# Delta-rule layer: a half-size inverse layout, and 512-column matmuls for every block but the gates

## The chip, the cores and the metric
The kernel runs on one core of one Trainium2 chip. The metric is the device time of one execution in microseconds (us). The kernel before takes 2532.01 us (median of 3 runs, 2531.71 to 2532.07). Five engines work side by side from queues of their own: TensorE (PE in the profile, its weight loads are PEld), VectorE (DVE), ScalarE (ACT), GpSimd (POOL) and SyncE (SP), which issues the weight transfers.

## The reference
Two layers over 256 tokens of width 2048, float32: differential attention and a gated MLP with a causal convolution, then a gated delta-rule layer and a second such MLP. Only the delta-rule layer changes. Its core, cut to what matters:

```python
proj = h @ w_in                                   # q, k, v, z, and two gate columns per head
qkv = silu(causal_dwconv(qkv, conv_w))            # 4 taps
q, k = l2_norm(q), l2_norm(k)
# per head and chunk of 64 tokens:
low = strict_lower(k_beta @ k.T * decay)
u, w = solve(I + low, v_beta), solve(I + low, k_beta * exp(g))
...                                               # scan over the 4 chunks with a state
o = rms_norm(o, norm_g) * silu(z)
x = x + o @ w_out
```

There are 16 q/k heads and 32 value heads of 128 columns. The kernel solves with an explicit inverse of unit lower triangular matrices: first all diagonal blocks of 32x32 by elimination on DVE, then the off-diagonal blocks by small matmuls.

## The kernel before, in words
Every large product is done in float32 precision with two halves of each operand. A weight chunk of 128x1024 numbers lands by DMA in `raw`; ACT rounds it to `whi` (L89) and DVE subtracts to get `wlo` (L90). The activations stand as a high half and a low half side by side, 2 x 256 columns. Each of `raw`, `whi`, `wlo` has four buffers.

`dense` (L132) multiplies one weight block of 256 output rows: for each of the k tiles and each of two row tiles it runs one *step*. A step in the **wide** form is two matmuls: high weights over all 512 activation columns (L151), whose low-activation half goes to its own 256 columns of the PSUM bank, and low weights over the 256 high-activation columns (L152). A step in the **narrow** form is three matmuls of 256 columns, all into the same 256 columns of PSUM: L151, L152, and the high weights loaded again for the low activations (L154). After a wide block the two column halves of the bank must still be added: in `lin` ACT copies the small half (L580), DVE adds the main half (L581) and scales by the row norm (L205); after a narrow block DVE scales directly out of PSUM (L196). In `out`, a wide block costs two additions to `x` on DVE (`add_x`, L343), a narrow one costs one. Two PSUM tiles `ps` take turns, so a block's bank pair must be read before the block after the next begins.

`gdn` (L542) goes through four groups of four q/k heads (b = 0..3). Per group: four `k` blocks (q and k of one head, 16 k tiles each), one `v` block, two `z` blocks in the other orientation (`dense_tok`, L207), three more `v` blocks, and then the eight output blocks of the group before (`out`, L818, 8 k tiles each). The last group's output blocks follow at the end.

All other work is spread between the weight chunks by generators: after every chunk `tick` (L71) advances each live generator to its next `yield`. So a `yield` means "one weight chunk later" in program order. `keys` (L594) squares and splits q and k, sums over the head by matmul, normalises, multiplies q and k and writes the diagonal blocks, by POOL copies (L650), into `Cc`. `invert` (L654) transposes `Cc` on DVE into `X` (L659), fills `Ti` with minus `X` and ones on the diagonal (L661, L662), runs 30 elimination steps of a multiply (L667) and a subtract (L670), and transposes the result twice (`ttc` L674, `tcc` L676). `levels` (L679) builds the larger inverse with small matmuls and POOL copies, and `group` (L752) applies it and makes the operand `oc` of the output blocks. A scheduler keeps program order as priority, with the compile-time readiness of each instruction; on the chip every engine runs its own list in the fixed order that results.

In `Ti`, 128 partitions hold four quadrants of 32 rows; the 32 partitions of a quadrant are 32 matrices, of which 16 are real (8 value heads x 2 half sequences) and 16 are zero. Elimination step j works on (31-j) x j numbers per partition.

Of the kernel before, what the change touches and what calls it, by code (L numbers as in the profile page):

```python
# [16 lines left out]
P = 128  # L17
T = 256
D = 2048
KD = D // P  # L20
# [6 lines left out]
class Trunk:  # L27
# [514 lines left out]
    def gdn(self, w_gate, w_in, w_z, w_out, nb, hb, gate_ap, const_ap, conv_col, ng, done):  # L542
# [7 lines left out]
        nc, tc, mp = self.nc, self.tc, self.mp  # L550
        nq = nb * hb
# [3 lines left out]
        with tc.tile_pool(name="gd", bufs=1) as gd:  # L555
# [3 lines left out]
            ident, mask = con[:, :P], con[:, P:]  # L559
# [9 lines left out]
                nc.gpsimd.memset(Tas[i][:64], 0.0)  # L569
            quad = [slice(32 * s, 32 * s + 32) for s in range(4)]  # L570
            flat = "p i c -> p (i c)"
            gates, lows = {}, []

            def lin(w, wide):
# [19 lines left out]
            def keys(hq, c, cc, b0, res):  # L594

                sq = gd.tile([P, 2, T], F32, tag="qs", name="qs", bufs=2)
                nc.scalar.square(sq, c)
                sp = gd.tile([P, 2, 2, T], F32R, tag="qp", name="qp", bufs=1)
                lows.append(self.split(sp, sq))

                def fetch():
                    d = gd.tile([P, 2, 384], F32, tag="lt", name="lt", bufs=hb)
                    nc.sync.dma_start(d, gates["rows"][2 * hq:2 * hq + 2, :].unsqueeze(0).to_broadcast([P, 2, 384]))
                    return d

                d = fetch() if "rows" in gates else None
                yield
                yield
                while "rows" not in gates:
                    yield  # L610
                if d is None:
                    d = fetch()
                    yield
                    yield
                    yield
                gc = gates["col"]
                dv = d[:, :, :T].rearrange("p v (t c) -> p v t c", t=2)
# [12 lines left out]
                nc.vector.tensor_tensor(c, c, sq, ALU.mult)  # L630
                q, k = c[:, 0, :], c[:, 1, :]
                yield
                yield
                prods = []
                for r in (k, q):
                    p = mp()
                    nc.tensor.matmul(p[:, :P], k[:, P:], r[:, P:], start=True, stop=True)
                    nc.tensor.matmul(p[:, P:384], k[:, :P], r, start=True, stop=True)  # L638
                    prods.append(p)
                lt = d  # L640
                qkt = gd.tile([P, 2, 384], F32, tag="qkt", name="qkt", bufs=hb)
                for v in range(2):
                    nc.vector.scalar_tensor_tensor(
                        qkt[:, v], prods[1][:, :384], P ** -0.5, d[:, v], ALU.mult, ALU.mult)
                    nc.vector.tensor_tensor(lt[:, v], prods[0][:, :384], d[:, v], ALU.mult)
                for v in range(2):
                    b = b0 + v
                    lv = lt[:, v, :T].rearrange("p (t c) -> p t c", t=2)
                    for r in quad:
                        nc.gpsimd.tensor_copy(  # L650
                            cc[r, :, 2 * b:2 * b + 2].rearrange("p c t -> p t c"), lv[r, :, r])
                    res.append((lt[:, v], qkt[:, v]))

            def invert(cc, lqs, inv):  # L654

                while len(lqs) < 2 * hb:
                    yield
                x = gd.tile([P, 32, 32], F32, tag="s4", name="X", bufs=3)
                nc.vector.transpose(x.rearrange(flat), cc.rearrange(flat))  # L659
                t = gd.tile([P, 32, 32], F32, tag="s4", name="Ti", bufs=3)  # L660
                nc.vector.tensor_scalar(t, x, -1.0, None, ALU.mult)  # L661
                nc.vector.memset(t.rearrange(flat)[:, ::33], 1.0)  # L662
                for j in range(1, 31):
                    m = 31 - j
                    tmp = gd.tile([P, T], F32, tag="tmp", name="tmp", bufs=1)
                    w = tmp[:, :m * j].rearrange("p (i c) -> p i c", c=j)
                    nc.vector.tensor_tensor(  # L667
                        w, x[:, j + 1:, j:j + 1].to_broadcast([P, m, j]),
                        t[:, j:j + 1, :j].to_broadcast([P, m, j]), ALU.mult)
                    nc.vector.tensor_tensor(t[:, j + 1:, :j], t[:, j + 1:, :j], w, ALU.subtract)  # L670
                    if j % 3:
                        yield
                ttc = gd.tile([P, 32, 32], F32, tag="s4", name="ttc", bufs=3)
                nc.vector.transpose(ttc.rearrange("p m i -> p i m"), t)  # L674
                tcc = gd.tile([P, 32, 32], F32, tag="s4", name="tcc", bufs=3)
                nc.vector.transpose(tcc.rearrange("p m c -> p c m"), t.rearrange("p i c -> p c i"))  # L676
                inv += [ttc, tcc]

            def levels(lqs, inv, gs, done):  # L679
# [137 lines left out]

            def out(b, acts):  # L818
                for blk in range(KD // 2):
                    wide = b == nb - 1 or blk >= KD // 4  # L820
                    ps = self.dense(w_out[b * (KD // 2) + blk], 2 * hb, lambda k: self.await_(acts, k), wide=wide)
                    self.add_out(blk, ps, done if b == nb - 1 else None, wide)

# [2 lines left out]
            pend = None  # L826
            for b in range(nb):
                heads = range(b * hb, (b + 1) * hb)
                cc = gd.tile([P, 32, 32], F32, tag="s4", name="Cc", bufs=3)
                nc.gpsimd.memset(cc, 0.0)  # L830
                lqs, inv, solved, acts, zts = [], [], [], [], {}
                groups = [range(i, i + gh) for i in range(0, hb, gh)]
                plan = [("k", i) for i in range(hb)] + [("v", 0)] + [("z", g) for g in range(len(groups))]
                for op, i in plan + [("v", i) for i in range(1, hb)]:
                    if op == "k":
                        hq = heads[i]
                        c = convs(lin(w_in[hq * 2], False), (hq, nq + hq))
                        self.spawn(keys(hq, c, cc, 2 * i, lqs))
                        if i == hb - 1:
                            self.spawn(invert(cc, lqs, inv))  # L840
                            self.spawn(levels(lqs, inv, range(len(groups)), solved))
                    elif op == "z":
                        gr = groups[i]
                        zt = zts[i] = gd.tile([P, 2, gv, P], F32, tag="vz", name="zt", bufs=4)
                        ps = self.dense_tok(w_z[heads[gr[0]] // 2], KD, self.h_acts)
                        for t in range(2):
                            nc.scalar.activation(zt[:, t].rearrange(flat), ps[:, t, :], AF.Silu,  # L847
                                                 scale=self.rstdc[:, t:t + 1])
                    else:
                        gi = i // gh  # L850
                        gr = groups[gi]
                        if i == gr[0]:
                            vt = gd.tile([P, 2, gv, P], F32, tag="vz", name="vt", bufs=4)
                            ready = []
                            self.spawn(group(gi, gr, lqs, solved, vt, ready, zts, acts))
                        hq = heads[i]
                        c = convs(lin(w_in[hq * 2 + 1], b<nb-1),
                                  (2 * nq + 2 * hq, 2 * nq + 2 * hq + 1))
                        self.spawn(to_tokens(c, vt, 2 * (i - gr[0]), ready))
                if pend:  # L860
                    out(*pend)
                pend = (b, acts)
# [213 lines left out]
```

## Time and profile before

| | |
|---|---|
| median of 3 runs | 2532.01 us |
| profiled execution | 2531.32 us, its span 2529.5 us |
| PE, PEld busy | 2522.4 us (100%), 2330.5 us (92%) |
| DVE, ACT, POOL busy | 1913.4 us (76%), 1501.8 us (59%), 97.2 us (4%) |
| chain that ended last | PE 99%, DMA 1% |
| weights read | 482.32 MB, 192 GB/s over the span |

In the lines of groups a row reads: line, engine, operation, output<-inputs, shapes, count | busy us in all, mean ns of one | idle time of the engine before them, and who ended it. Matmuls are pipelined: a matmul's own duration in the profile is longer than the distance to the next one, so the cost of a step is read from the distance between starts in the timeline. The delta-rule layer lies between about 1050 us and 1850 us of the span.

### The profile page before, as it was taken

Reading aid. Unit: us, or ns where it says so; the run is one execution under the profiler, and the core shown is the slowest. Engines: PE = TensorE matmul, PEld = TensorE weight load, DVE = VectorE, ACT = ScalarE, POOL = GpSimd, SP = SyncE. Lnnn points to the kernel's source line nnn. Section 1 sums busy time; section 2 is a strip of 40 time slices with the busy share of each in tenths; the row PEclk is TensorE's granted clock in tenths of the full one; section 3 lists DMA queues with packets and bytes.
Section 4 is the critical chain, followed back from the end, with each engine's and each line's share of the span. In section 5 each row is a group of like instructions: output and inputs, shape, how many; then the busy total and the mean of one; then the engine's idle time right before and its main releaser. Section 6 shows DMA issues by size and latency. Waiting matters only on the chain.

```text
span 2529.5 us, 42709 instructions
## 1 busy us (share of the span) xinstructions
PE 2522.4 (100%) x16727; PEld 2330.5 (92%) x16727; DVE 1913.4 (76%) x2822; ACT 1501.8 (59%) x2082; POOL 97.2 (4%) x189
## 2 busy tenths in 40 slices
PE   9999999999999999999999999999999999999999
PEld 8998899999999999999989989999999999999998
DVE  8886677777777555689879789788787777776544
ACT  7766656666666444485674675674566666665343
POOL 0000000000000000011110021021000000000000
PEclk9999999999999999999999999999999999999999
DMA  7555566666666666666555555555466666666665
GB/s 257 175 183 175 167 204 201 201 201 201 201 201 202 201 199 201 203 189 207 163 170 197 162 183 190 163 186 174 162 201 200 202 201 201 201 202 205 210 207 157
DMA packets 138203, 487.25 MB, mean 193 GB/s; under 512 B 15473, under 2 KB 18449, under 8 KB 138001
## 3 DMA queue, kind: packets, MB, share of 16 engines
q1 hardware_dynamic: 137712, 484.17, 60.0%
q8 instruction: 131, 2.15, 0.4%
q14 instruction: 72, 0.58, 0.1%
q10 hardware_dynamic: 288, 0.35, 0.0%
HBM read 482.32 MB, written 2.15 MB: 192 GB/s over the span
## 4 chain that ended last, share of the span: by engine, by line
PE 99%; DMA 1%; DVE 0%; ACT 0%; SPq 0%; issue 0%; ACTq 0%
PE ps L151 50%; PE ps L152 27%; PE ps L154 4%; PE ps L221 3%; PE ps L220 3%; PE ps L222 3%; PE mp L765 2%; PE mp L151 1%; PE mp L329 1%; PE mp L638 1%; PE mp L152 0%; PE ps L123 0%; PE mp L730 0%; PE mp L748 0%; PE mp L810 0%; PE mp L466 0%
## 5 line engine op out<-in xcount | busy, mean ns | idle before, releaser
L90 DVE TENSOR_TENSOR wlo<-raw,whi 128x1024 fp32r<-128x1024 f32 (+2 forms) x911 | 1102.6, 1212 | 510.2 <-ACT whi L89 502.0
L89 ACT CAST whi<-raw 128x1024 fp32r<-128x1024 f32 (+2 forms) x911 | 944.1, 1038 | 849.9 <-PE ps L151 627.1
L151 PE MATMUL ps<-h,whi 128*128 128x512 f32 (+1 forms) x4208 | 1348.0, 366 | 0.0
L152 PE MATMUL ps<-h,wlo 128*128 128x256 f32 x4208 | 1151.2, 274 | 0.6 <-DVE wlo L90 0.6
L151 PEld LDWEIGHTS ps<-h,whi 128*128 128x128 f32 x4208 | 797.2, 189 | 93.6 <-ACT zt L847 0.2
L152 PEld LDWEIGHTS ps<-h,wlo 128*128 128x128 f32 x4208 | 807.7, 192 | 2.0 <-DVE wlo L90 0.9
L151 PE MATMUL ps<-ac,whi 128*128 128x512 f32 x1546 | 506.8, 382 | 0.0
L152 PE MATMUL ps<-ac,wlo 128*128 128x256 f32 x1546 | 421.2, 273 | 0.0
L151 PEld LDWEIGHTS ps<-ac,whi 128*128 128x128 f32 x1546 | 292.1, 189 | 40.6 <-PE ps L151 0.2
L152 PEld LDWEIGHTS ps<-ac,wlo 128*128 128x128 f32 x1546 | 296.8, 192 | 0.1
L154 PE MATMUL ps<-h,whi 128*128 128x256 f32 x656 | 181.8, 277 | 0.0
L151 PE MATMUL ps<-oc,whi 128*128 128x512 f32 (+1 forms) x512 | 159.7, 344 | 0.0
L220 PE MATMUL ps<-whi,h 128*128 128x512 f32 x384 | 146.4, 381 | 0.0
L221 PE MATMUL ps<-wlo,h 128*128 128x512 f32 x384 | 145.8, 380 | 0.0
L222 PE MATMUL ps<-whi,h 128*128 128x512 f32 x384 | 145.8, 380 | 0.0
L310 DVE SCALAR_TENSOR_TENSOR cv<-u,fcols,cv 128x255 f32<-128x255 f32 (+1 forms) x344 | 142.9, 477 | 0.0
L152 PE MATMUL ps<-oc,wlo 128*128 128x256 f32 x512 | 140.7, 275 | 0.0
L154 PEld LDWEIGHTS ps<-h,whi 128*128 128x128 f32 x656 | 125.8, 192 | 0.2
L151 PEld LDWEIGHTS ps<-oc,whi 128*128 128x128 f32 x512 | 97.4, 190 | 8.0
L152 PEld LDWEIGHTS ps<-oc,wlo 128*128 128x128 f32 x512 | 98.3, 192 | 0.3
L308 ACT ACTIVATE cv<-u,fcols 128x256 f32<-128x256 f32 x172 | 93.9, 593 | 0.6 <-DVE u L205 0.5
L310 DVE SCALAR_TENSOR_TENSOR cv<-u,cols,cv 128x255 f32<-128x255 f32 (+2 forms) x192 | 84.2, 478 | 0.4 <-ACT cv L306 0.3
(222 smaller groups left out, 2178.7 us busy)
## 6 DMA issues: line engine op xcount, KB each, us to landing
raw<-w_up SPq DMA_DIRECT2D x344, 512.0 KB, 4.7
raw<-w_down SPq DMA_DIRECT2D x160, 512.0 KB, 3.7
raw<-w_in SPq DMA_DIRECT2D x128, 512.0 KB, 4.6
raw<-w_z SPq DMA_DIRECT2D x64, 512.0 KB, 3.8
raw<-w_out SPq DMA_DIRECT2D x64, 512.0 KB, 4.3
raw<-w_qk SPq DMA_DIRECT2D x56, 512.0 KB, 4.6
raw<-w_v SPq DMA_DIRECT2D x32, 512.0 KB, 3.5
raw<-w_o SPq DMA_DIRECT2D x32, 512.0 KB, 4.7
```

What stands on the lines that cost most here:

```text
L89: self.cast = nc.scalar.copy(hi[:, :, s], raw[:, :, s])
L90: nc.vector.tensor_tensor(lo[:, :, s], raw[:, :, s], hi[:, :, s].bitcast(F32), ALU.subtract)
L151: nc.tensor.matmul(bank[c][:, :n], hi[:, k, s], self.turns(a[:, :n // T, :]), start=first, stop=False)
L152: nc.tensor.matmul(bank[c][:, :T], lo[:, k, s], self.turns(a[:, :1, :]), start=False, stop=last and wide)
L154: nc.tensor.matmul(bank[c][:, :T], hi[:, k, s], self.turns(a[:, 1:, :]), start=False, stop=last)
L220: nc.tensor.matmul(ps[:, c, :], ah, wh, start=first, stop=False)
L221: nc.tensor.matmul(ps[:, c, :], ah, wl, start=False, stop=False)
L222: nc.tensor.matmul(ps[:, c, :], al, wh, start=False, stop=last)
L308: nc.scalar.activation(out, u, AF.Identity, bias=bias, scale=taps[n - 1])
L310: nc.vector.scalar_tensor_tensor(out[:, j:], u[:, :T - j], taps[n - 1 - j], out[:, j:], ALU.mult, ALU.add)
L329: last = self.nc.tensor.matmul(out, self.onesr, self.pairs(p[:, j]), start=i + j == 0, stop=i + j == n)
L765: nc.tensor.matmul(p[:, v, :], l(v), r[:, v, :], start=i == 0, stop=i == len(terms) - 1)
```

## The change
Two things change in `gdn`.

First, the inverse. `Cc` holds only the 16 real matrices per quadrant (`nl = 4 * hb`). The transpose into `X` reads them twice over, so that partitions 0 to 15 of a quadrant and partitions 16 to 31 hold the same 16 matrices. `Ti` is 32x16: the first half of the partitions holds the even columns of the inverse, the second half the odd ones. Elimination step j, now for j = 0..30, works on (31-j) x (j//2+1) numbers. `Ti` starts as a unit pattern (a POOL memset of 512 columns and two POOL copies of 16 columns from a small tile `half`, which DVE makes once), so the fill by DVE goes. The final transposes are of 512 columns instead of 1024, and `ttc` is made from `tcc`. The memset of `Cc` goes. Each of these tiles gets a buffer of its own where five shared three.

Second, the widths. All `k` blocks, the last group's `v` blocks, and the first four output blocks of groups 0 to 2 go from narrow to wide. Only the gate block stays narrow. `keys` waits one more `yield` before it goes on.

```diff
@@ keys
-                yield
-                yield
+                for _ in range(3):
+                    yield
@@ invert
+                while not lqs:
+                    yield
+                if b == 0:
+                    nc.vector.tensor_reduce(half, ident.rearrange("p (q a c) -> p a q c", q=4, a=2), AX.XY, ALU.add)
+                t = gd.tile([P, 32, 16], F32, tag="Ti", name="Ti")
+                nc.gpsimd.memset(t, 0.0)
+                for a in range(2):
+                    nc.gpsimd.tensor_copy(t.rearrange(flat)[:, 16 * a::33], half[:, a:a + 1].to_broadcast([P, 16]))
                 while len(lqs) < 2 * hb:
                     yield
-                x = gd.tile([P, 32, 32], F32, tag="s4", name="X", bufs=3)
-                nc.vector.transpose(x.rearrange(flat), cc.rearrange(flat))
-                t = gd.tile([P, 32, 32], F32, tag="s4", name="Ti", bufs=3)
-                nc.vector.tensor_scalar(t, x, -1.0, None, ALU.mult)
-                nc.vector.memset(t.rearrange(flat)[:, ::33], 1.0)
-                for j in range(1, 31):
-                    m = 31 - j
+                x = gd.tile([P, 32, 32], F32, tag="X", name="X")
+                nc.vector.transpose(x, cc.unsqueeze(2).to_broadcast([P, 32, 2, nl]))
+                for j in range(31):
+                    m, n = 31 - j, j // 2 + 1
...
-                ttc = gd.tile([P, 32, 32], F32, tag="s4", name="ttc", bufs=3)
-                nc.vector.transpose(ttc.rearrange("p m i -> p i m"), t)
-                tcc = gd.tile([P, 32, 32], F32, tag="s4", name="tcc", bufs=3)
-                nc.vector.transpose(tcc.rearrange("p m c -> p c m"), t.rearrange("p i c -> p c i"))
+                tcc = gd.tile([P, nl, 32], F32, tag="tcc", name="tcc")
+                nc.vector.transpose(tcc.rearrange("p m (c a) -> p c a m", a=2), t.rearrange("p i c -> p c i"))
+                ttc = gd.tile([P, nl, 32], F32, tag="ttc", name="ttc")
+                nc.vector.transpose(ttc.rearrange(flat), tcc.rearrange(flat))
@@ out
-                    wide = b == nb - 1 or blk >= KD // 4
+                    wide = True
@@ the loop over groups
-                cc = gd.tile([P, 32, 32], F32, tag="s4", name="Cc", bufs=3)
-                nc.gpsimd.memset(cc, 0.0)
+                cc = gd.tile([P, 32, nl], F32, tag="Cc", name="Cc")
...
-                        c = convs(lin(w_in[hq * 2], False), (hq, nq + hq))
+                        c = convs(lin(w_in[hq * 2], True), (hq, nq + hq))
...
-                        c = convs(lin(w_in[hq * 2 + 1], b<nb-1),
+                        c = convs(lin(w_in[hq * 2 + 1], True),
```

More of the change, by code (lines that the diff above doesn't have):

```diff
@@ L571, in gdn @@
             flat = "p i c -> p (i c)"
+            nl = 4 * hb
+            half = gd.tile([P, 2], F32, tag="half", name="half")
             gates, lows = {}, []
@@ L652, in keys, with invert @@
                     res.append((lt[:, v], qkt[:, v]))
-            def invert(cc, lqs, inv):
+            def invert(b, cc, lqs, inv):
+                while not lqs:
[6 more added lines that the diff above has]
+                    nc.gpsimd.tensor_copy(t.rearrange(flat)[:, 16 * a::33], half[:, a:a + 1].to_broadcast([P, 16]))
@@ L665, in invert @@
+                nc.vector.transpose(x, cc.unsqueeze(2).to_broadcast([P, 32, 2, nl]))
+                for j in range(31):
+                    m, n = 31 - j, j // 2 + 1
                     tmp = gd.tile([P, T], F32, tag="tmp", name="tmp", bufs=1)
-                    w = tmp[:, :m * j].rearrange("p (i c) -> p i c", c=j)
+                    w = tmp[:, :m * n].rearrange("p (i c) -> p i c", c=n)
                     nc.vector.tensor_tensor(
-                        w, x[:, j + 1:, j:j + 1].to_broadcast([P, m, j]),
-                        t[:, j:j + 1, :j].to_broadcast([P, m, j]), ALU.mult)
@@ L670, in invert @@
-                    nc.vector.tensor_tensor(t[:, j + 1:, :j], t[:, j + 1:, :j], w, ALU.subtract)
+                        w, x[:, j + 1:, j:j + 1].to_broadcast([P, m, n]),
+                        t[:, j:j + 1, :n].to_broadcast([P, m, n]), ALU.mult)
+                    nc.vector.tensor_tensor(t[:, j + 1:, :n], t[:, j + 1:, :n], w, ALU.subtract)
                     if j % 3:
                         yield
-                ttc = gd.tile([P, 32, 32], F32, tag="s4", name="ttc", bufs=3)
-                nc.vector.transpose(ttc.rearrange("p m i -> p i m"), t)
@@ L836, in gdn @@
                         hq = heads[i]
-                        c = convs(lin(w_in[hq * 2], False), (hq, nq + hq))
+                        c = convs(lin(w_in[hq * 2], True), (hq, nq + hq))
                         self.spawn(keys(hq, c, cc, 2 * i, lqs))
                         if i == hb - 1:
-                            self.spawn(invert(cc, lqs, inv))
+                            self.spawn(invert(b, cc, lqs, inv))
                             self.spawn(levels(lqs, inv, range(len(groups)), solved))
```

## The prediction
> **What bounds the kernel now.** I read the head of the page first (what is busy, what ended last), then the groups kept apart by shape, then the waits within the delta-rule layer, then the timeline of PE.
>
> ```profile
> span 2529.5 us, 42709 instructions
> PE 2522.4 (100%) x16727; PEld 2330.5 (92%) x16727; DVE 1913.4 (76%) x2822; ACT 1501.8 (59%) x2082; POOL 97.2 (4%) x189
> PE 99%; DMA 1%; DVE 0%; ACT 0%; SPq 0%; issue 0%; ACTq 0%
> ```
>
> PE is the bound, and the chain that ended last is PE from end to end. Whether the other engines ever hold it up in this layer stands in the waits between 1040 and 1850 us (PE's whole list, and the largest of ACT and DVE):
>
> ```profile
> PE ps L152 <- DVE wlo L90: 0.6, 1, 0.6
> ACT whi L89 <- PE ps L151: 83.5, 60, 2.8
> ACT whi L89 <- PE ps L154: 73.3, 51, 2.9
> DVE wlo L90 <- ACT whi L89: 76.9, 71, 3.3
> ```
>
> PE shows one wait for a weight half, 0.6 us. The casts wait for PE to free a buffer, 157 us in the first two rows. So the weights run ahead, and DVE time freed by the smaller inverse is by itself worth nothing: nothing on PE waits for it. What the change can gain must come from PE's own steps, so these are counted and timed.
>
> ```profile
> L151 PE MATMUL ps<-h,whi 128*128 128x256 f32 x656 | 181.9, 278 | 0.0
> L154 PE MATMUL ps<-h,whi 128*128 128x256 f32 x656 | 181.8, 277 | 0.0
> L154 PE MATMUL ps<-oc,whi 128*128 128x256 f32 x192 | 53.1, 276 | 0.0
> ```
>
> The narrow steps are the L154 matmuls: 656 + 192 = 848. The gate block keeps 16 (one row tile, 16 k tiles), so 832 steps change: 16 k blocks and 4 v blocks of 32 steps, 12 output blocks of 16.
>
> **The change part by part.** *PE.* The column "mean" is a pipelined duration and would mislead: by it a narrow step costs 3 x 277 = 831 ns and a wide one 382 + 274 = 656. Starts tell the truth. Output blocks of group 0, first narrow, then wide, in one timeline:
>
> ```profile
> 1355.05 0.28 PE L151 MATMUL ps<-oc,whi 128*128 128x256 f32 x1
> 1355.16 0.28 PE L152 MATMUL ps<-oc,wlo 128*128 128x256 f32 x1
> 1355.28 0.28 PE L154 MATMUL ps<-oc,whi 128*128 128x256 f32 x1
> 1355.39 0.28 PE L151 MATMUL ps<-oc,whi 128*128 128x256 f32 x1
> ...
> 1367.11 0.28 PE L151 MATMUL ps<-oc,whi 128*128 128x256 f32 x1
> ...
> 1371.80 0.38 PE L151 MATMUL ps<-oc,whi 128*128 128x512 f32 x1
> ...
> 1385.88 0.38 PE L151 MATMUL ps<-oc,whi 128*128 128x512 f32 x1
> 1386.10 0.27 PE L152 MATMUL ps<-oc,wlo 128*128 128x256 f32 x1
> 1386.21 0.38 PE L151 MATMUL ps<-oc,whi 128*128 128x512 f32 x1
> ...
> 1389.81 0.38 PE L151 MATMUL ps<-oc,whi 128*128 128x512 f32 x1
> ```
>
> From 1355.05 to 1367.11 there are 36 narrow steps: 12.06 / 36 = 335.0 ns. From 1371.80 to 1389.81 there are 55 wide ones: 18.01 / 55 = 327.5 ns. The columns streamed are the same (768); a step saves 7.5 ns, and 832 x 7.5 = **6.24 us**. In both stretches starts are evenly spaced, so this is PE's own pace and no wait is in it.
>
> The Trainium skill (TensorE: Matmul & The Clock Gate, section "Back-to-back issue gap") puts an isolated matmul at its columns over 2.4 GHz plus 2.5 ns. That would be 327.5 ns for the narrow step and 325.0 for the wide, a gain of 2.5 ns a step or an estimated 2.1 us. The trace agrees within 1% on the wide step (327.5) and not on the narrow one (335.0).
>
> *DVE and ACT, widths.*
>
> ```profile
> L580 ACT COPY u<-ps 128x512 f32<-128x512 f32 x12 | 6.9, 576 | 0.0
> L581 DVE TENSOR_TENSOR u<-ps,u 128x512 f32<-128x512 f32 x12 | 8.2, 682 | 0.0
> L205 DVE TENSOR_TENSOR u<-u,rstd 128x512 f32<-128x512 f32 x98 | 67.7, 691 | 2.9
> L196 DVE TENSOR_TENSOR u<-ps,rstd 128x512 f32<-128x512 f32 x20 | 13.7, 686 | 2.2 <-PE ps L154 2.1
> L343 DVE TENSOR_TENSOR x<-ps,x 128x512 f32<-128x512 f32 x98 | 67.3, 687 | 10.3 <-PE ps L152 6.9 <-PE ps L154 2.1
> ```
>
> Each of the 20 k and v blocks gains a copy on ACT (0.58 us, 11.5 in all) and on DVE 682 + 691 - 686 = 687 ns; each of the 12 output blocks gains one L343 (687 ns). DVE: 32 x 0.687 = 22.0 us. A block's convolution input is ready 0.58 + 0.69 = 1.26 us later.
>
> *DVE, inverse.* One group's share, and the shortest and longest elimination steps:
>
> ```profile
> L667 DVE TENSOR_TENSOR tmp<-X,Ti 128x30 f32<-128x30 f32 (+14 forms) x30 | 9.8, 327 | 0.6
> L670 DVE TENSOR_TENSOR Ti<-Ti,tmp 128x30 f32<-128x30 f32 (+14 forms) x30 | 9.8, 327 | 0.4
> L667 DVE TENSOR_TENSOR tmp<-X,Ti 128x240 f32<-128x240 f32 x2 | 0.8, 406 | 0.0
> L667 DVE TENSOR_TENSOR tmp<-X,Ti 128x30 f32<-128x30 f32 x2 | 0.4, 178 | 0.0
> L676 DVE STREAM_TRANSPOSE tcc<-Ti 128x1024 f32<-128x1024 f32 x4 | 8.4, 2088 | 0.0
> L674 DVE STREAM_TRANSPOSE ttc<-Ti 128x1024 f32<-128x1024 f32 x4 | 8.1, 2016 | 0.0
> L659 DVE STREAM_TRANSPOSE X<-Cc 128x1024 f32<-128x1024 f32 x4 | 5.0, 1243 | 2.0 <-POOL Cc L650 2.0
> L661 DVE TENSOR_SCALAR Ti<-X 128x1024 f32<-128x1024 f32 x4 | 2.7, 686 | 0.0
> ```
>
> Before: 19.6 us of elimination, 4.1 of closing transposes, 0.7 of filling. A line through 178 and 406 ns gives 145 ns plus 1.09 ns a number; the sum of (31-j)(j//2+1) is 2856 numbers in 31 steps, so 2 x (31 x 0.145 + 2856 x 0.00109) = 15.2 us after (halving the numbers does not halve the time: the 145 ns stay). Transposes of half the size: an estimate of 1.0 + 0.6 by half of L676 and of L659. So 24.4 becomes 16.8, about 7.6 us less a group, 30 us in all; X with its repeated input I leave at 1.24 (2.1 at worst, by L676). DVE's net is near -8 us, but not in one place: the k blocks get +2.7 us a group and the saving falls in the stretch of the v and output blocks behind them. On POOL a memset of 1024 columns goes and smaller ones come; POOL is 4% busy. The one-time reduction for `half` (128 columns) I bound by the 0.69 us of a 512-column pass. On PE none of this counts as long as the weight halves arrive ahead.
>
> *The thin place.* The margin is smallest in the first z block of a group, when the norms of the last k heads, the exponentials and the group before all meet on ACT:
>
> ```profile
> 1275.70 1.04 ACT L89 CAST whi<-raw 128x1024 fp32r<-128x1024 f32 x1
> 1276.65 0.58 ACT L580 COPY u<-ps 128x512 f32<-128x512 f32 x1
> 1277.05 1.22 DVE L90 TENSOR_TENSOR wlo<-raw,whi 128x1024 fp32r<-128x1024 f32 x1
> 1278.18 0.69 DVE L581 TENSOR_TENSOR u<-ps,u 128x512 f32<-128x512 f32 x1
> 1271.21 0.27 PE L152 MATMUL ps<-h,wlo 128*128 128x256 f32 x1
> 1279.31 0.38 PE L221 MATMUL ps<-wlo,h 128*128 128x512 f32 x1
> 1113.22 0.38 PE L152 MATMUL ps<-h,wlo 128*128 128x256 f32 x1 [0.57 <-DVE wlo L90]
> ```
>
> The low half made until 1278.27 is used at 1279.31: a margin of 1.0 us in group 1. Group 0 has none: PE waits 0.57 us at 1113. The copy and add of the last k block would push there, 1.26 us. Against that, program order puts `keys` one chunk (eight steps, 2.6 us) later, which spreads the same heap. Bounds on PE: from -0.6 (the one wait goes) to +1.26 us in each of four groups, +5.0. I take +0.5, nearest to the waits row, where 800 us hold a single one.
>
> *The later inverse.* One chunk later, everything behind `keys` moves 2.6 us. Group 0 to 2 results are used a whole group later; in the last group, sixteen chunks of the output blocks of group 2 (some 42 us) lie between. I cost it at 0; were that cover gone, 2.6 us once.
>
> *Sum.* Profiled execution 2531.32 (span 2529.5 and 1.8 around it) - 6.24 + 0.5 = 2525.6. The median stands 0.69 us above that execution, so **2526.3 us**.
>
> **The rivals.** *Waits eat the gain.* The extra 1.26 us reaches PE in two to four groups, at the chunk shown above. For it: margins of 1.0 and 0. Against: the later `keys`, and ACT's 157 us of waiting on PE. Time: 2532.0 - 6.2 + 2.5 to 5.0 = 2528.3 to 2530.8.
>
> *Slower: the PSUM banks come free too late.* A wide block frees its bank only after a copy on ACT and an add on DVE, each in its engine's order behind casts. Above, the v block's last matmul starts at 1271.21, its copy at 1276.65 and its add ends at 1278.87: 7.7 us. The next k block but one starts one block, 32 x 0.3275 = 10.5 us, after; a narrow block needs only one DVE operation. From 10.5 us of delay on PE stops. If the last two k blocks and the v block of each group overrun by 1 us: 12 us, 2532.0 - 6.2 + 12 = 2537.8. Against: 2.8 us of room even here, and earlier k blocks meet less work. The Trainium skill (PSUM — Partial Sum Buffer, section "Engine vs sequencer instructions") calls the ACT and DVE queues strictly first-in first-out, which is what lets a late copy hold up the casts behind it; the timeline above, with the cast at 1275.70 ahead of the copy, shows such an order but not its price.
>
> *The width doesn't pay.* If the 0.11 us spacing of the narrow rows came from waits or from the mix of neighbours, nothing would be won: 2532. Against it: 36 steps evenly at 335.0 ns. The page on TensorE named above leads to nearly this case, 2529.9 by its figures.
>
> **How the numbers follow.** Under 0.2% (5.1 us) I call a change the same, about what can be told from no change here. Forecast, gain with at most 1.1 us of waits, to 2526.9: 0.50, and that is all of faster. Waits eat the gain: 0.33; the width doesn't pay: 0.04; together same, 0.37. Banks: 0.13, slower. The likeliest case alone spans 2525.2 to 2526.9. The range for 8 in 10 takes in the waits rival, some of the slower one, and below the forecast 2 us for small gaps at the switches of form that I can't price: 2523.6 to 2533.0.
>
> **What would show it.** After: no L154 but the gate's 16; L151 starts 0.3275 us apart in k blocks; L667 and L670 near 7.6 us a group each, 31 of each; L580 x32; PE's waits on L90 or L89 in this layer below 1.5 us. The prediction is wrong if PE waits there add up to several us, if L151 waits for an L581 or L343 (a bank), or if narrow k blocks turn out to have run faster than 335 ns.

## The result

The changed kernel takes **2535.59 us** (median of 21 runs, 2534.49 to 2538.09) against 2531.94 us for the kernel before, measured beside it (21 runs, 2530.75 to 2534.40): ratio 1.0015 with a 95% interval of 1.0009 to 1.0021. It is 3.7 us slower. That is inside the 0.2% band called "the same" above, but the interval excludes no change, the sign is opposite to the forecast of 5.7 us faster, and the time lies 2.6 us above the top of the range given (2533.0).

The page of the changed kernel, its head and the engines' shares of the chain that ended last:

```profile
span 2534.0 us, 41116 instructions
PE 2521.1 (99%) x15895; PEld 2304.1 (91%) x15895; DVE 1913.0 (75%) x2855; ACT 1513.8 (60%) x2104; POOL 98.0 (4%) x197
PE 94%; ACT 3%; DVE 1%; issue 1%; DMA 1%; ACTq 0%
```

PE has 832 matmuls fewer and is busy 1.3 us less, yet the span is 4.5 us longer (2529.5 before). The chain tells why: it was PE for 99% and is now PE for 94%. PE is made to wait.

First the part that went as planned. Groups by shape between 1040 and 1860 us, and a k block in PE's timeline:

```profile
L151 PE MATMUL ps<-h,whi 128*128 128x512 f32 x1045 | 346.6, 383 | 0.0
L154 PE MATMUL ps<-h,whi 128*128 128x256 f32 x16 | 4.4, 275 | 0.0
L582 ACT COPY u<-ps 128x512 f32<-128x512 f32 x32 | 18.5, 577 | 0.1
```

```profile
1079.75 0.38 PE L151 MATMUL ps<-h,whi 128*128 128x512 f32 x1
...
1084.01 0.38 PE L151 MATMUL ps<-h,whi 128*128 128x512 f32 x1
```

Only the gate's 16 matmuls of L154 are left, the copies are 32 (L580 of before is L582 now), and 13 wide steps of a k block take 4.26 us: 327.7 ns each. The 6.24 us were there.

Now the waits of PE in the same 820 us. Before, this list held one wait of 0.6 us:

```profile
PE ps L221 <- DVE wlo L90: 1.9, 2, 1.1
PE ps L152 <- DVE wlo L90: 1.8, 1, 1.8
PE ps L151 <- DVE oc L821: 1.3, 2, 0.8
PE mp L329 <- ACT qp L321: 1.0, 2, 0.5
PE mp L884 <- DVE glin L196: 1.0, 1, 1.0
PE ps L220 <- ACT whi L89: 0.4, 1, 0.4
```

Together 7.4 us. PE loses somewhat more than this list counts: taken as the distance between two starts less the usual distance, the same nine waits cost 9.1 us, and the one of before 0.7. The delta-rule layer, from the first matmul of the gate block to the end of the last output block, takes 799.5 us after 794.9. All other stages keep their length to 0.1 us, except that the program's first 50 us vary by up to 1.4 us from one profile to the next, whatever the kernel. So the layer's +4.6 us has to be explained, and this is the account:

| term | us |
|---|---|
| 832 steps at 7.5 ns | -6.2 |
| head of the layer: `wlo` late for L152 (2.0), gate block's row `glin` late for L884 (1.1) | +3.1 |
| group 0's z blocks and what stands just ahead of them: 3.0 after, 0.7 before | +2.2 |
| last output blocks, L151 for their operand `oc` | +1.7 |
| key sums (squares summed over the head in `keys`; L329 waits for their split, `qp`), groups 2 and 3 | +1.3 |
| small 32x32 matmuls in `levels`, which came in another order | +1.9 |
| sum; the rest, 0.6, was not tracked down | +4.0 |

**The head of the layer** shows the largest single wait. DVE in the kernel after, then in the kernel before, then PE after:

```profile
1055.27 0.68 DVE L343 TENSOR_TENSOR x<-ps,x 128x512 f32<-128x512 f32 x1
1059.52 0.29 DVE L661 TENSOR_REDUCE half<-con 128x2 f32<-128x128 f32 x1 [3.57 <-DMA con<-const]
1059.73 1.22 DVE L90 TENSOR_TENSOR wlo<-raw,whi 128x1024 fp32r<-128x1024 f32 x1
```

```profile
1055.35 0.68 DVE L343 TENSOR_TENSOR x<-ps,x 128x512 f32<-128x512 f32 x1
1056.56 1.23 DVE L90 TENSOR_TENSOR wlo<-raw,whi 128x1024 fp32r<-128x1024 f32 x1 [0.53 <-ACT whi L89]
```

```profile
1061.00 0.38 PE L152 MATMUL ps<-h,wlo 128*128 128x256 f32 x1 [1.84 <-DVE wlo L90]
```

The one-time reduction that makes `half` stands late in the program, but its only input is a constant, and in DVE's list it came out at the front of this layer. There DVE sits idle for 3.57 us until that constant's DMA lands, with a weight half behind it that was ready to be made at 1056.56 before.

**The small matmuls** are no wait in the list at all. `levels` makes two products per head pair with them: `px` (L716 before, L723 after), which reads `ttc`, and `py` (L718, L725), which reads `TT`, a copy of parts of `ttc` that POOL makes. PE in group 2, before and after (starts; before, the two alternate x, x, y in what is left out):

```profile
1572.18 0.22 PE L716 MATMUL mp<-ttc,pc 32*32 32x32 f32 x2
...
1573.32 0.48 PE L151 MATMUL ps<-oc,whi 128*128 128x512 f32 x1
```

```profile
1555.57 0.67 PE L723 MATMUL mp<-ttc,pc 32*32 32x32 f32 x32
1556.17 0.38 PE L152 MATMUL ps<-oc,wlo 128*128 128x256 f32 x1
...
1557.03 0.69 PE L725 MATMUL mp<-pc,TT 32*32 32x32 f32 x16
1557.64 0.38 PE L152 MATMUL ps<-oc,wlo 128*128 128x256 f32 x1
```

Before, 96 small matmuls of both head pairs (64 `px`, 32 `py`) stand interleaved and take 1.14 us, 48 of them 0.57. After, the second pair's 32 `px` take 0.60 us by themselves, and its 16 `py` come 0.86 us later and take another 0.61. A group loses some 0.6 us; three of the four groups do.

### The profile page after: what moved, and what is told of

Its sections match the earlier page's. It is cut to its first block, busy times and chain, and to the rows that moved or that the text cites. A ratio compares the mean times of both kernels' runs of the same rounds, so it can differ in the third digit from the quotient of the medians.

```text
span 2534.0 us, 41116 instructions
## 1 busy us (share of the span) xinstructions
PE 2521.1 (99%) x15895; PEld 2304.1 (91%) x15895; DVE 1913.0 (75%) x2855; ACT 1513.8 (60%) x2104; POOL 98.0 (4%) x197
## 4 chain that ended last, share of the span: by engine, by line
PE 94%; ACT 3%; DVE 1%; issue 1%; DMA 1%; ACTq 0%
PE ps L151 51%; PE ps L152 26%; PE ps L221 3%; PE ps L222 3%; PE ps L220 3%; PE mp L772 2%; PE mp L151 1%; ACT whi L89 1%; PE ps L123 1%; PE mp L329 1%; PE mp L152 0%; DVE wlo L90 0%; ACT L593 0%; ACT L297 0%; PE mp L640 0%
## 5 line engine op out<-in xcount | busy, mean ns | idle before, releaser
L151 PE MATMUL ps<-h,whi 128*128 128x512 f32 x4208 | 1383.4, 382 | 0.0
L152 PE MATMUL ps<-h,wlo 128*128 128x256 f32 x4208 | 1150.8, 273 | 1.8 <-DVE wlo L90 1.8
L151 PEld LDWEIGHTS ps<-h,whi 128*128 128x128 f32 x4208 | 795.4, 189 | 109.4
L152 PEld LDWEIGHTS ps<-h,wlo 128*128 128x128 f32 x4208 | 807.7, 192 | 3.7 <-DVE wlo L90 2.0
L151 PE MATMUL ps<-ac,whi 128*128 128x512 f32 x1546 | 506.8, 382 | 0.0
L152 PE MATMUL ps<-ac,wlo 128*128 128x256 f32 x1546 | 421.2, 273 | 0.0
L151 PEld LDWEIGHTS ps<-ac,whi 128*128 128x128 f32 x1546 | 292.1, 189 | 40.7 <-PE ps L151 0.2
L152 PEld LDWEIGHTS ps<-ac,wlo 128*128 128x128 f32 x1546 | 296.8, 192 | 0.1
L151 PE MATMUL ps<-oc,whi 128*128 128x512 f32 x512 | 170.9, 384 | 1.3 <-DVE oc L821 1.3
L152 PE MATMUL ps<-oc,wlo 128*128 128x256 f32 x512 | 142.2, 278 | 0.0
L151 PEld LDWEIGHTS ps<-oc,whi 128*128 128x128 f32 x512 | 96.8, 189 | 14.3 <-DVE oc L821 1.8
L152 PEld LDWEIGHTS ps<-oc,wlo 128*128 128x128 f32 x512 | 98.2, 192 | 0.6
L343 DVE TENSOR_TENSOR x<-ps,x 128x512 f32<-128x512 f32 x110 | 75.8, 689 | 13.1 <-PE ps L152 11.5
L205 DVE TENSOR_TENSOR u<-u,rstd 128x512 f32<-128x512 f32 x118 | 81.5, 691 | 3.3
```

Source lines behind the costliest of these rows:

```text
L151: nc.tensor.matmul(bank[c][:, :n], hi[:, k, s], self.turns(a[:, :n // T, :]), start=first, stop=False)
L152: nc.tensor.matmul(bank[c][:, :T], lo[:, k, s], self.turns(a[:, :1, :]), start=False, stop=last and wide)
L205: self.nc.vector.tensor_tensor(u, u, self.rstd.unsqueeze(1).to_broadcast([P, u.shape[1], T]), ALU.mult)
L343: self.nc.vector.tensor_tensor(x, part, x, ALU.add)
```

## The experiments

Each row of the table is the median against the kernel before as measured beside it (2531.6 us in the first four rows, 2532.0 in the next four, 2532.2 in the next three, 2531.9 in the last). "Layer" is the length of the delta-rule layer in the profiled execution, 794.9 us before and 799.5 after; it leaves out the variable start of the program. The profiled execution is not always one near the median: late_two's took 2538.12 us, outs_only's 2536.55, best_old_inverse's 2554.58, and their layers are to be read with that.

| run | median, us | ratio to before, 95% interval | layer, us |
|---|---|---|---|
| late_half | 2533.16 | 1.0006 [0.9997, 1.0014] | 797.1 |
| widths_only | 2542.54 | 1.0045 [1.0033, 1.0058] | 806.2 |
| inverse_only | 2533.52 | 1.0008 [0.9999, 1.0017] | 797.1 |
| outs_only | 2535.78 | 1.0015 [1.0006, 1.0024] | 799.5 |
| late_quad | 2530.61 | 0.9995 [0.9986, 1.0003] | 794.7 |
| late_quad_v | 2530.41 | 0.9995 [0.9986, 1.0004] | 794.1 |
| late_quad_k | 2531.47 | 0.9998 [0.9989, 1.0006] | 794.9 |
| late_two | 2536.58 | 1.0018 [1.0010, 1.0027] | 801.5 |
| inverse_quad | 2531.24 | 0.9997 [0.9988, 1.0006] | 795.1 |
| quad_v_four | 2529.92 | 0.9991 [0.9982, 1.0000] | 793.4 |
| quad_v_four_k | 2528.58 | 0.9986 [0.9977, 0.9995] | 792.6 |
| best_old_inverse | 2558.68 | 1.0110 [1.0094, 1.0127] | 818.5 |

### The reduction for `half`, moved back (late_half)

```diff
 # invert, on the changed kernel
-                    nc.vector.tensor_reduce(half, ...)
+                    with tc.issue_after(lows[-1].ins):      # behind the first keys' low half
+                        nc.vector.tensor_reduce(half, ...)
```

> The changed kernel with one edit: the one-time reduction for `half` (L661) is ordered on DVE behind the first heads' split of the squares instead of floating to the head of the layer. Theory A (the trace after: DVE sits 3.57 us in front of this reduction, waiting for the constants to land, and PE then waits 2.0 us at 1058.9 and 1.1 us at 1072.6): 3.1 us less than the changed kernel, 2532.5 us. Theory B (the wait is only where a shortage shows that exists anyway, the waits move on to the next blocks): within 0.7 us of the changed kernel, 2535.6 us.

The layer is 2.4 us shorter and the time 2533.2 us. The reduction now stands at 1132.64 us. Three of PE's five waits in the layer:

```profile
PE ps L221 <- DVE wlo L90: 1.9, 2, 1.1
PE ps L151 <- DVE oc L822: 1.3, 2, 0.8
PE mp L885 <- DVE glin L196: 0.5, 1, 0.5
```

L152's wait is gone and the gate row's is halved; the others are untouched. So one operation of 0.29 us had cost the changed kernel 2.4 us. The kernel is still not faster than before.

### The two halves of the change, each alone (inverse_only, widths_only, outs_only)

inverse_only is the kernel before with the new inverse and its late `half`; widths and the two yields stay as they were. widths_only is the kernel before with every block but the gates wide and three yields. outs_only is the kernel before with one line:

```diff
 # out
-                    wide = b == nb - 1 or blk >= KD // 4
+                    wide = True
```

> The new inverse alone with the widths and the two yields of before, and with the reduction for `half` ordered late. Theory A (nothing on PE waits for the DVE time that the smaller inverse frees): 2531.9 us, within 0.7 us of before. Theory B (the freed DVE time is worth something on PE): 2529 us or less.

> The kernel before with the widths alone: all k, v and output blocks wide, three yields in `keys`, the old inverse. Theory A (the wide steps gain 6.2 us on PE, and the later, fuller ACT and DVE queues in the k and z blocks and at the last output blocks give back 5 us, whatever the inverse): 2530.7 us, PE waits in the layer of some 5 us, none of them at a `half`. Theory B (the inverse's new order is what makes PE wait): 2525.7 us and PE waits under 1.5 us.

> The kernel before with one edit: all output blocks wide; 192 steps change. Theory A (7.5 ns a step, and a stretch with margin): 1.4 us less than before, 2530.5 us. Theory B (the second addition to x on DVE, 12 x 0.69 us where DVE is already 95 to 100% busy with the old inverse, makes the weights late): 2532 us or more, with PE waits on wlo between 1345 and 1390.

inverse_only met neither expectation, at 1.9 us above before: the smaller inverse by itself gains nothing and loses a little. Its elimination and closing transposes (the changed kernel's rows, four groups):

```profile
L677 DVE TENSOR_TENSOR Ti<-Ti,tmp 128x126 f32<-128x126 f32 (+22 forms) x124 | 31.6, 255 | 2.8
L674 DVE TENSOR_TENSOR tmp<-X,Ti 128x126 f32<-128x126 f32 (+22 forms) x124 | 31.5, 254 | 2.8
L681 DVE STREAM_TRANSPOSE tcc<-Ti 128x512 f32<-128x512 f32 x4 | 4.5, 1132 | 0.0
L683 DVE STREAM_TRANSPOSE ttc<-tcc 128x512 f32<-128x512 f32 x4 | 2.8, 698 | 0.0
```

That is 15.8 us of elimination and 1.8 us of transposes a group, as worked out beforehand (15.2 and 1.6). The DVE time is really saved; PE gains nothing from it.

widths_only missed both expectations by more than ten us. Its largest waits:

```profile
PE mp L810 <- DVE zt L799: 2.4, 1, 2.4
PE mp L730 <- DVE Ta L736: 2.3, 1, 2.3
PE ps L151 <- DVE oc L814: 2.3, 1, 2.3
```

All three lie in the last group, where DVE has the inverse, the larger inverse (`Ta`), the gating (`zt`) and the output operand (`oc`) to finish while little other work of PE is left to cover them. late_half differs from widths_only in the inverse alone and is 9.4 us faster. Not all of that is waiting: in widths_only PE's granted clock is 0.50 from 1803.9 to 1810.7 and from 1821.0 to 1824.4 us, in and behind such waits (last section). PE is busy for 9.0 us of these stretches, so up to 4.5 us go there; late_half has no such stretch in the layer. So DVE time freed by the inverse is worth nothing next to the old widths, and 9 us next to the new ones, half of it perhaps through the clock. The two halves of the change are not additive.

outs_only changes 12 output blocks and is 4.2 us slower than before, where the steps alone would have saved 12 x 16 x 7.5 ns = 1.4 us. That is theory B's time, but not its place or its wait. Its largest waits:

```profile
PE ps L151 <- DVE oc L814: 2.3, 1, 2.3
PE ps L151 <- DVE x L343: 1.8, 2, 1.4
```

The second row is a PSUM bank that comes free too late, the slower rival of the prediction; 1.7 us more are lost behind it at half clock (last section). The changed kernel has no such wait in its list. That the smaller inverse is the reason is not shown: widths_only keeps the old inverse, has the same wide output blocks, and has no wait for a bank either.

### The order of POOL's copies (late_quad, inverse_quad)

Why did the `py` matmuls of the second head pair come late? They read a quadrant of `TT`, which POOL copies from `ttc`. POOL in group 0, before and after:

```profile
1207.46 5.55 POOL L698 COPY TT<-ttc 32x256 f32<-32x256 f32 x8 [58.41 <-DVE ttc L674]
1213.05 1.91 POOL L700 COPY Ta<-tcc 32x256 f32<-32x256 f32 x4
```

```profile
1196.59 2.03 POOL L707 COPY Ta<-tcc 32x256 f32<-32x256 f32 x4 [41.57 <-DVE tcc L681]
1198.67 0.53 POOL L663 MEMSET Ti<- 128x512 f32 x1
1199.27 5.17 POOL L705 COPY TT<-ttc 32x256 f32<-32x256 f32 x8
```

`ttc` used to be made first; now it is made from `tcc`, and POOL starts with the four `Ta` copies and the next group's memset, and the eight `TT` copies are last. The edit copies the quadrant that `py` needs for both head pairs before the rest:

```diff
 # levels
+                for g in gs:
+                    nc.gpsimd.tensor_copy(TTs[g][quad[1], :, quad[1]], ttc[quad[1], nm * g:nm * g + nm, :])
                 for g in gs:
                     ms = slice(nm * g, nm * g + nm)
-                    for s in (1, 3, 0, 2):
+                    for s in (3, 0, 2):
```

> Made from the changed kernel with the late `half`; one edit more: in `levels`, POOL copies quadrant 1 of both head pairs' TTs before anything else, so that the second pair's small `py` matmuls find their operand when `px` of the same pair is done. Theory A (the small 32x32 matmuls of `levels` cost 1.5 to 2 us more because they stand in two bursts instead of interleaved, and the burst comes from the order in which POOL's copies are ready): px and py interleave again and the time is 1.5 us below late_half, 2531.7 us. Theory B (the order of the small matmuls follows something else, or the bursts are not dearer): 2533.2 us, as late_half.

> The smaller inverse alone (all widths and the two yields of `keys` as in the kernel before, late `half`), with quadrant 1 of both TTs copied first: inverse_only plus that one edit. Theory A (the 1.9 us that inverse_only lost to the kernel before is the order of the small `px` and `py` matmuls): 2.0 to 2.5 us below inverse_only, 2531.3 us, the time of the kernel before; the inverse itself is worth nothing, since its DVE time lies beside PE. Theory B (the loss of inverse_only lies elsewhere, and the gain of late_quad came from another effect of the POOL copies): 2533.5 us, as inverse_only.

Both went as theory A said, late_quad by more: its layer is 2.4 us shorter than late_half's, and inverse_quad's is 2.1 us shorter than inverse_only's, at 2531.24 us against 2531.3 expected. In late_quad 96 small matmuls again take 1.14 us (1550.83 to 1551.97, x, x, y throughout). So the loss of inverse_only was the order of these small matmuls, and the new inverse next to the old widths is worth nothing that can be told (0.9997, interval 0.9988 to 1.0006).

### The places where PE still waits (late_quad_v, late_quad_k, late_two)

```diff
 # late_quad_v, on late_quad
-                        c = convs(lin(w_in[hq * 2 + 1], True),
+                        c = convs(lin(w_in[hq * 2 + 1], b<nb-1),
 # late_quad_k, on late_quad
-                        c = convs(lin(w_in[hq * 2], True), (hq, nq + hq))
+                        c = convs(lin(w_in[hq * 2], b>0), (hq, nq + hq))
 # late_two, on late_half
-                for _ in range(3):
+                for _ in range(2):
```

> As late_quad, and the v blocks of the last group run narrow again (4 blocks less 1: 3 wide in the other groups stay, the 4 v blocks of the last group go back, which is what the kernel before did differently there: 4 x 32 steps x 7.5 ns = 0.96 us is given back). Theory A (the two waits of 1.7 us on L151 for the last group's gathered outputs come from DVE and ACT being late in the last group, to which the four extra copies and adds, 4 x 0.69 us on DVE, belong): the 1.7 us go, 0.96 us come, net 0.7 us below late_quad. Theory B (the waits come from the inverse, which ends a chunk later, not from the v blocks): the waits stay and the time is 1.0 us above late_quad.

> As late_quad, and the four k blocks of group 0 run narrow again (4 x 32 steps x 7.5 ns = 0.96 us is given back, the other twelve k blocks stay wide). Theory A (PE's waits at the first z blocks of group 0, 2.2 us more than before, come from the copy on ACT and the add on DVE that a wide k block adds just ahead of them): those waits fall to 0.7 us or less, net 1.2 us below late_quad. Theory B (they come from the inverse's new place or from the exponentials and the casts themselves): the waits stay near 2.3 us and the time is 1.0 us above late_quad.

> The changed kernel with the late `half`, and `keys` yields twice instead of three times, as in the kernel before: the third yield is the one thing undone. Theory A (the third yield takes the norms and key sums away from the heap at the first z block): without it PE's waits on the weight halves and on the key sums (L329) grow by 1 us or more and the time is at least 1 us above late_half, 2534.2 us or more. Theory B (a chunk earlier or later makes no difference, or the later keys are what makes PE wait 1.0 us on L329 and 1.7 us at the last output blocks): 2531 to 2533.2 us, the same as late_half or below it.

late_quad_v: the layer is 0.6 us shorter, as theory A said, and no wait on `oc` is left; the medians differ by only 0.2 us. Four wide v blocks bought 0.96 us of steps and cost 1.7 us at the end.

late_quad_k: the waits of the z blocks went, and others of the same size came. Its list begins

```profile
PE mp L639 <- DVE cv L632: 1.4, 1, 1.4
```

and this row, at 1268 us in group 1, does not stand in late_quad's list. The layer is 0.2 us longer than late_quad's and the median 0.9 us higher: theory A's waits and nearly theory B's time. The wide k blocks did cause the waits on the weight halves, but taking all four back only moved the loss.

late_two: the third yield is worth some 3 us: the median is 4.6 us above before, late_half's 1.6. (The layers differ by 4.4, but late_two's profiled execution was 1.5 us above its median, with a stretch of 3.6 us at a clock of 0.59 in it.) Its time is theory A's, but the waits on the key sums, which A expected to grow, are gone. What grew are others: the weight halves are late three times, once by 2.3 us in group 1 (the thin place of the prediction), and the output operand once:

```profile
PE ps L221 <- DVE wlo L90: 4.1, 3, 2.3
PE ps L151 <- DVE oc L822: 2.3, 1, 2.3
```

### A faster version (quad_v_four, quad_v_four_k, best_old_inverse)

```diff
 # quad_v_four, on late_quad_v
-                for _ in range(3):
+                for _ in range(4):
 # quad_v_four_k, on quad_v_four: the two blocks ahead of group 0's first z block narrow
-                        c = convs(lin(w_in[hq * 2], True), (hq, nq + hq))
+                        c = convs(lin(w_in[hq * 2], b > 0 or i < 3), (hq, nq + hq))
...
-                        c = convs(lin(w_in[hq * 2 + 1], b<nb-1),
+                        c = convs(lin(w_in[hq * 2 + 1], 0 < b < nb - 1 or (b == 0 and i > 0)),
```

> As late_quad_v, and `keys` yields four times instead of three. Theory A (the two waits of the key sums on the cast qp, 1.1 us together, and part of the 2.0 us at group 0's z blocks come from `keys` still being too early for ACT, as two yields cost 3.4 us more than three): 1 to 1.5 us below late_quad_v, 2529.2 us. Theory B (three is already late enough; a fourth only moves the work of `keys` to another place, where as much is waited for, or later work of the last group ends later): 2530.4 us or up to 2 us above.

> As quad_v_four, and of group 0 the last k block and the v block behind it, the two blocks ahead of the first z block, run narrow (2 x 32 steps x 7.5 ns = 0.48 us is given back). Theory A (only the copies and adds of these two blocks fall into the heap at the z block): the waits on the weight halves there, 2.0 us, fall to 0.7 us or less, net 0.8 us below quad_v_four. Theory B (as with all four k blocks narrow, one wait goes and another of the same size comes): 0.5 us above quad_v_four, at most equal.

> As quad_v_four_k (four yields, the same six blocks narrow), but with the inverse of the kernel before: widths_only with the fourth yield and those six blocks narrow. Theory A (the smaller inverse pays only as room on DVE behind the wide blocks, and without it DVE is late for the last group's inverse, zt and oc, 7 us of waits in widths_only, four of which go with the narrow v blocks of the last group, 2.7 us of DVE): 2533 to 2537 us, still at least 4 us above quad_v_four_k. Theory B (what made widths_only slow was the heap of keys and the last group's v blocks, both mended here; the smaller inverse is not needed): 2530 us or less, within 1.5 us of quad_v_four_k.

quad_v_four is 0.5 us below late_quad_v in the median and 0.8 us in the layer: half of what theory A gave; one of the two waits on `qp` went, the z blocks' stayed. quad_v_four_k's time went as theory A said, or better: 0.7 us shorter in the layer and 1.3 us below quad_v_four in the median. The waits on the weight halves fell only from 2.0 to 1.0 us in the list. Its list in the layer:

```profile
PE ps L221 <- DVE wlo L90: 1.0, 1, 1.0
PE mp L329 <- ACT qp L321: 0.7, 1, 0.7
PE mp L887 <- DVE glin L196: 0.5, 1, 0.5
PE mp L639 <- DVE cv L632: 0.2, 1, 0.2
```

At 2528.58 us it is 3.6 us faster than the kernel before (0.9986, interval 0.9977 to 0.9995) and 7 us faster than the changed one. It gives back six blocks, 6 x 32 x 7.5 ns = 1.4 us of the steps.

best_old_inverse, the same with the old inverse, is 30 us slower than that, far beyond theory A's 4. In the profiled execution the layer is 25.9 us longer than in quad_v_four_k, and three causes are visible.

One is an order, not work. In groups 1 to 3 PE waits about 3 us each, 9.3 in all, for z's activation on ACT, because that activation stands behind a copy (L749) whose input PE makes late. ACT's timeline in group 1, where ACT itself sits idle at the copy:

```profile
1317.89 0.58 ACT L749 COPY vt<-mp 128x512 f32<-128x512 f32 x1 [3.07 <-PE mp L748]
```

In quad_v_four_k the copy stands ahead of the activation too, but PE has its input ready earlier, and it starts at 1307.14. Why PE's list came out so is not known.

The other two are in the last stage, from the output blocks of group 2 to the end of the layer: 119.9 us against 100.8. There the old inverse ends too late, as in widths_only: PE waits 7.8 us, where quad_v_four_k has no wait. Besides, PE runs at half clock from 1797.4 to 1814.4 us and is busy for 14.2 us of them, so up to 7.1 us go there. The rest was not tracked down. In the windows view the clock is the third figure from the end:

```profile
1800.00:1820.00 20.00, 18.03 (x131) 16.46 (x131) 4.13 (x6) 4.01 (x7) 0.00 (x0) 0.64 0.07 24
```

The four executions show the same: the lower the mean granted clock, 0.996 to 0.993, the longer the time, 2554.6 to 2562.6 us. So the run agrees with the wide blocks needing the smaller inverse, but it does not say by how much: the order and the clock have a part in the 30 us.

## Why the prediction was wrong

**Right: the steps.** 832 steps changed and a wide step takes 327.7 ns in a k block. The "width doesn't pay" rival is out. The Trainium skill (TensorE: Matmul & The Clock Gate, section "Back-to-back issue gap") leads to an estimate of 325.0 for the wide step; the trace keeps to 327.7.

**Wrong: "+0.5 waits" in the sum.** The step of the argument that failed is the sentence that on PE none of this counts "as long as the weight halves arrive ahead", and the price of +0.5 us that came from it. Measured are 8.4 us of waits more than before (9.1 against 0.7) and 1.9 us in the small matmuls. The weight halves did not all arrive ahead (4.2 of the 8.4 us), and PE turned out to wait for other things too. By its parts:

- *"The one-time reduction for `half` ... I bound by the 0.69 us of a 512-column pass."* It took 0.29 us and cost 2.4 us (late_half). I priced its duration and did not ask when its input lands nor where a scheduler puts an operation whose only input is a constant. Its duration was no bound for its cost: the weight half that stood behind it waited those 3.57 us too.
- *The thin place.* The first z block was the right place, but in one group only: 2.2 us more in group 0, where I had found no margin, and nothing in groups 1 to 3. The bounds of -0.6 to +5.0 held it; the value taken, "+0.5, nearest to the waits row", was the row of a kernel without the extra work. The third yield, which I counted as spreading the heap, is worth some 3 us (late_two): without it the thin place of group 1 does lose 2.3 us.
- *"The later inverse ... I cost it at 0; were that cover gone, 2.6 us once."* The cover was gone in part: 1.7 us on `oc` at the last output blocks. late_quad_v removes this wait with narrow v blocks in the last group and leaves the inverse a chunk later, and in late_two, with `keys` a chunk earlier, PE still waits 2.3 us for `oc`. So the four wide v blocks are what it takes, and a later inverse alone does not explain it; that it is their added copies and additions is argued. The prediction did not weigh them against the end of the layer.
- *Not in the sum at all:* the order of `ttc` and `tcc`, which changes when POOL copies `TT` and so the order of PE's small matmuls (1.9 us, and 2.4 us when mended), and the key sums of groups 2 and 3 (1.3 us; no run isolates them, but with two yields, in late_two, both waits are gone, so the third yield has a part in them). The prediction counted POOL by its load, 4%, not by its order.

**The rivals.** "Waits eat the gain" had the mechanism; its 2528.3 to 2530.8 was too low because it knew one place out of four. "Banks free too late" did not happen in the changed kernel, but did in outs_only, for 1.8 us; what makes the difference stays open.

**"DVE time freed by the smaller inverse is by itself worth nothing."** True as it stands: inverse_quad, 0.9997. But the conclusion drawn from it, that the inverse can be left out of the sum, was wrong for the pair: without it the wide blocks cost 9.4 us more (late_half against widths_only), lost clock included.

## What to carry to other kernels

When PE is busy 99% of the time, price a change by the new waits, not only by PE's steps: list every added operation with the arrival of its inputs and its neighbours in its engine's list, and look for operations that depend on nothing but a constant, since a scheduler may put them in front of work that is needed now, as it did here. A small engine's order (here POOL's copies at 4% load) can set the order of matmuls, so a swap of two results is a change to check on PE. And the uniform rule ("all blocks wide") was not the best one here: leaving six of the 64 k, v and output blocks narrow, mending two orders and moving one generator by a yield turned +3.7 us into -3.6.

## What the hardware showed that was not expected

The granted clock of PE can fall to about half after a wait of some two microseconds. The windows view of outs_only, a wait for a bank and the 3.6 us behind it, then a longer wait of the same run and what follows it, and last what follows that longer wait in widths_only; the clock is the third figure from the end:

```profile
1756.00:1758.20 2.20, 0.81 (x7) 0.58 (x6) 2.20 (x3) 0.58 (x1) 2.09 (x3) 1.00 0.51 145
1758.20:1761.80 3.60, 3.60 (x14) 3.11 (x13) 2.70 (x5) 0.70 (x2) 2.60 (x4) 0.53 0.71 225
...
1814.80:1817.40 2.60, 0.33 (x4) 0.09 (x2) 2.60 (x4) 1.58 (x3) 0.00 (x0) 1.00 0.27 77
1817.40:1821.00 3.60, 3.60 (x22) 3.31 (x23) 0.63 (x2) 0.14 (x1) 0.00 (x0) 1.00 0.71 237
1821.00:1825.00 4.00, 4.00 (x14) 3.49 (x15) 0.58 (x1) 0.00 (x0) 0.00 (x0) 0.58 0.67 213
```

In the second row the wide matmuls start 427 ns apart instead of 218, so the stretch does about half its work: 3.6 x (1 - 0.53) = 1.7 us more are lost. The distance between the two starts around the wait was 1.66 us. The next two rows are a longer one of the same run, 2.55 us, with no such stretch behind it. The last row stands behind the same wait in widths_only, as long and for the same operand, and there the clock drops. So the length of the wait does not decide it. late_two shows the drop after 2.72 us (clock 0.59), the changed kernel none after 2.12 us. What else decides, no run here settles. A wait can therefore cost more than its length: up to 4.5 us more in widths_only and up to 7.1 in the 17 us stretch of best_old_inverse.

The other is the price of small matmuls by their order: 16 `py` of 32x32 by themselves take 0.61 us, 38 ns each, while as every third of a row of `px` they come at one in 36 ns together with two `px`. That they overlap with their neighbours is measured; that it is because `px` and `py` use different quadrants of the array is only a guess.
